# A two-layer trunk: token-major residual, nine seven-product units and a per-token shift in the first feed-forward block

## The chip, the core and the metric

One core of one Trainium2 chip runs the kernel. The metric is the device time of one execution in microseconds, as a median of several runs. Engines are named as in the profile: PE is TensorE, whose weight loads are shown as PEld; DVE is VectorE, ACT is ScalarE, POOL is GpSimd, SP is SyncE, which here issues DMAs. L164 means line 164 of the kernel.

## What is computed

A decoder trunk of two layers over one sequence of 256 tokens with 2048 features, in float32. Layer 0 mixes tokens by trailing means; layer 1 by attention in three dilated branches, with keys and values made of layer 0's output. Each layer ends in a gated feed-forward block (FFN) with a causal convolution of width 3 and 5504 hidden features, and each half ends in a layer norm over `ALPHA * h + f(h)`:

```
def conv_ffn(h, w_up, conv_w, conv_b, w_down):
    u = h @ w_up
    ...
    gate, val = jnp.split(c, 2, axis=-1)
    return (jax.nn.silu(gate) * val) @ w_down
...
        h = layer_norm(DEEPNORM_ALPHA * h + mix, ln1_g[i], ln1_b[i])
        ff = conv_ffn(h, ffn_w_up[i], ffn_conv_w[i], ffn_conv_b[i], ffn_w_down[i])
        h = layer_norm(DEEPNORM_ALPHA * h + ff, ln2_g[i], ln2_b[i])
```

The change touches `ff` of layer 0, the addition that follows, and the norm behind it.

## The kernel before, in words

**Units.** All weights pass through a list of units (`units`). A unit is a block of at most 512 x 512 weights with a function that issues its matmuls and one that runs behind them (`post`). `run_units` works through the list in order. Ahead of each unit, `ahead` issues the weight loads of up to five units to come on SP (L72) and splits those of up to three: ACT casts a block to fp32r (`wh`, L82), DVE takes the rest (`wl`, L83). Three raw buffers and four pairs of split ones bound this. A product of two float32 matrices is then three fp32r products: high by high, high by low, low by high. `later(n, f)` runs `f` behind the matmuls of the unit that comes n units later. So the order on every engine is the order in which the Python code issues instructions; each engine works strictly in its order, and a wait on one instruction holds back all behind it.

**Feature-major groups** (`group`, `mm_quad`, L149-186). Four row blocks of weights (three in the FFN's last down stage) add up into four PSUM banks, one for each 128 output features, with tokens along the free axis. In mode "ab" a matmul of 512 columns multiplies `wh` by the high and low part of the activations side by side, and one of 256 multiplies `wl` by the high part (L164, L165). Modes "a" and "x" take three matmuls of 256 or 258 columns (L167-169).

**Token-major groups** (`group_tm`, L188-268) hold 128 tokens in the partitions and 512 output features along the free axis: two PSUM banks, 24 matmuls of 512 columns for 512 rows of weights (L230-232).

**Seven block products.** In layer 1's FFN some units of the down projection use a scheme with seven products of half blocks in place of eight (`mk_seven`, L194-222; the table is `sevens`, L560). Such a unit takes two turns, "a" and "b", with 42 matmuls of 256 columns in all (L219-221). The weights' sums are made by DVE in `split_sums` (L90-108: two splits, L103, four sums, L105-108, and the split of the sums, L96); the activations' sums by `left_sums` (L619). Its results are put onto the residual by `early_post` (L724), in part by accumulating DMAs on POOL (L260).

**The FFN** (`ffn`, L556-697). It has eleven blocks q of 512 hidden features (the last has 384), each with a gate group and a value group of four row blocks. After blocks 2, 5, 7 and 10 comes a down stage over the blocks since the last one: three, three, two and three row blocks for each of the four groups c of 512 output features. The first two groups of a stage are interleaved (`turns`): a0 a1 b0 a2 b1 b2, then c0 c1 c2, d0 d1 d2. In layer 0 the down groups are feature-major: `resid_add` (L302) adds the PSUM banks to the residual H. In layer 1 the residual is moved to token-major layout at the FFN's start by `to_tokens` (L703: a DVE transpose of 32 x 32 blocks, L708, then sixteen DMAs on SP for the places of the blocks, L717), once for each c, and `tm_post` (L746) adds to it.

**The norm behind layer 0's FFN.** The last down stage runs `resid_last` (L315). For numerical safety a shift is taken off the residual ahead of the statistics: the mean over group 0's features, from a matmul with ones (`shift`, L364), which DVE subtracts from group 0, and which for the other groups enters their PSUM banks by one more matmul with `neg1` (L171). `stats` (L359) squares a group on ACT (L343) and folds it and its square over the free axis on DVE (L347, L349, L352). `xp` (L391) multiplies the not yet normalised residual by the norm's gain and splits it (L396, L397): it is what the first K group multiplies, one quarter for each of its four units, and the normalisation is applied behind that group (`norm_evac`, L443, L450, L452). `chain` (L402) sums the folds over partitions with two matmuls (L403, L404), makes the mean and the reciprocal deviation (L408-412), and then normalises the four quarters (L417, L418, L424) and splits them (L426, L274) into the operands XC, with which the query projection begins.

**Masks.** Three times, 30, 32 and 34 units behind the start of layer 0's FFN, `masks` (L1052) makes a 128 x 128 mask for the attention: an iota on POOL and ten DVE instructions (L1060-1067).

Of the kernel before, what the change touches and what calls it, by code (L numbers as in the profile page):

```python
# [32 lines left out]
def trunk(ctx: ExitStack, tc: tile.TileContext, x, pool_w_in, pool_w_grp, pool_scale, pool_w_out,  # L33
# [115 lines left out]
    def mm_quad(xq, ps, first, last, mode, mid, shifted):  # L149
        def go(h, l):  # L150
# [9 lines left out]
            for i, (k, m) in enumerate(order):  # L160
                c = slice(m * P, (m + 1) * P)
                st, sp = first and k == 0, last and k == nk - 1
                if mode == "ab":
                    PE.matmul(ps[m], h[:, k, c], q[:, k, :, :T], start=st, stop=False)  # L164
                    PE.matmul(ps[m][:, :T], l[:, k, c], q[:, k, 0, :T], start=False, stop=sp and not shifted)  # L165
                else:
                    PE.matmul(ps[m][:, :n], h[:, k, c], q[:, k, 0, :n], start=st, stop=False)  # L167
                    PE.matmul(ps[m][:, :n], h[:, k, c], q[:, k, 1, :n], start=False, stop=False)  # L168
                    PE.matmul(ps[m][:, :n], l[:, k, c], q[:, k, 0, :n], start=False, stop=sp and not shifted)  # L169
                if sp and shifted:  # L170
                    PE.matmul(ps[m][:, :T], neg1, ST["cs"], start=False, stop=True)  # L171
# [4 lines left out]
    def group(w, r0s, c0, ncol, xqs, post, mode="ab", mids=(), shifted=False):  # L176
        ps = []
        for j, (r0, nr) in enumerate(r0s):
            last = j == len(r0s) - 1
            units.append((w[r0:r0 + nr, c0:c0 + ncol],  # L180
                          mm_quad(xqs[j], ps, j == 0, last, mode, mids[j] if j < len(mids) else None, shifted),
                          (lambda: post(ps)) if last else None))
# [5 lines left out]
    def group_tm(w, r0s, c0, ncol, xqs, post, apart=False, seven=None, early=None):  # L188
# [5 lines left out]
        def mk_seven(kind):  # L194
            fin = len(r0s) == 2

            def go(h, l):
# [7 lines left out]
                def sm(i):  # L205
                    return lambda hl, kk: seven()[i][:, hl, kk, :]
# [82 lines left out]
    neg1 = const.tile([P, P], F32R, name="neg1")  # L289
# [12 lines left out]
    def resid_add(c, first):  # L302
        def post(ps):
            for m in range(4):
                y = H[c][:, m, :]
                if first:
                    V.scalar_tensor_tensor(y, y, ALPHA, ps[m][:, :T], op0=OP.mult, op1=OP.add)
                else:
                    V.tensor_tensor(y, y, ps[m][:, :T], OP.add)
            for m in range(4):  # L310
                y = H[c][:, m, :]
                V.tensor_tensor(y, y, ps[m][:, T:], OP.add)
        return post

    def resid_last(c, first, lay, which, after):  # L315
        def post(ps):
            for m in range(4):
                y = H[c][:, m, :]
                if first and c == 0:
# [7 lines left out]
            if c == 0:  # L327
                s = fold(H[0], None, "S0", F32R)
                later(1, lambda: shift(s, first, lay, which))
# [34 lines left out]
    def shift(s, first, lay, which):  # L364
        ps = bank("shift")
        PE.matmul(ps[:, :T], ones4, s, start=True, stop=True)
        cs = lnp.tile([P, T], F32R, name="cs", tag="cs")
        A.copy(cs, ps[:, :T])
        ST["cs"] = cs
        cb = cs.bitcast(F32).unsqueeze(1).to_broadcast([P, 4, T])  # L370
        ST["S"] = ST["Q"] = None

        def one():
            V.tensor_tensor(H[0], H[0], cb, OP.subtract)
            if first:
                pre(1)
            stats(0)

        def two():
            xp(0, lay, which)  # L380
            if first:
                pre(2)
                pre(3)
# [76 lines left out]
    def add_resid(w, rows, srcs, first):  # L460
        for c in range(4):
            group(w, rows, 512 * c, 512, srcs, resid_add(c, first))

    def add_last(w, rows, srcs, first, lay, which, after=None):
        for c in range(4):
            group(w, rows, 512 * c, 512, srcs, resid_last(c, first, lay, which, after),
                  mode="a" if c == 3 else "ab", shifted=c > 0 and not first)
# [66 lines left out]
    def add_grp(g):  # L534
# [12 lines left out]
             True, 0, 0)  # L547
# [8 lines left out]
    def ffn(lay):  # L556
# [3 lines left out]
        sevens = {0: (1, (0, 1, 2, 3)), 3: (4, (0, 1, 2, 3)), 6: (7, (2,)), 8: (9, (0, 2))} if lay == 1 else {}  # L560
# [58 lines left out]
        def left_sums(q, s):  # L619
            two = lnp.tile([P, 2, 2, 2, P], F32R, name="xs01", tag="sq")  # L620
            one = pools["ffn"].tile([P, 2, 2, P], F32R, name="xs2", tag="xs", bufs=1)
            if any(v[0] == q and len(v[1]) < 4 for v in sevens.values()):
                if "xs3" not in ST:
                    ST["xs3"] = hp.tile([P, 2, 2, 2, P], F32R, name="xs3", tag="h")
                own = ST["xs3"][:, 0]
            else:
                own = gq[q][:, 0:2, :, P:T].rearrange("p k h t -> p h k t")
# [479 lines left out]
```

## Time and profile before

| what | us |
|---|---|
| median of 3 runs | 2061.72 (2060.78 to 2063.05) |
| span of the profiled execution, first to last instruction | 2060.0 |
| PE busy | 2049.6 |
| DVE busy | 1505.6 |
| ACT busy | 1032.9 |
| POOL busy | 36.5 |

For the profiled execution the page gives the span alone. Matmuls overlap, and the ends of matmuls are modelled, so the time of a stage of PE's work is read from the start of its first matmul to the start of the first of the next stage. By this the first FFN's four down stages begin at 351.86, 554.18, 711.51 and 880.28 us of the span, and the K projection begins at 943.98. The second FFN's down stages begin at 1464.60, 1666.36, 1820.80 and 1988.38.

A row of the table of stretches has: the stretch, its length, PE's busy time in it with the number of matmuls that touch it, the granted clock, the share of the DMA engines' time and GB/s. A row of the timeline has: start, length, engine, line, operation, output and inputs, shapes, count. A row of waits has: who waited for whom, us in total, times, the longest.

### The profile page before, as it was taken

How to read it: one execution, taken by the hardware profiler on the slowest of the kernel's cores; microseconds unless marked ns; L12 is line 12 of the kernel's file. 1: busy time of each engine (PE TensorE's matmuls, PEld its weight loads, DVE VectorE, ACT ScalarE, POOL GpSimd, SP SyncE). 2: the span in 40 equal slices, each digit the busy share in tenths (PEclk: the TensorE clock that was granted, in tenths of full speed). 3: DMA queues.
4: the chain of work that ended last, by engine and by line, in shares of the span. 5: the costliest groups of instructions: out<-in, count | busy, mean ns of one | idle time of the engine just before them, and what ended most of it. 6: DMA issues, size and time to landing. Idle time of an engine off the chain costs nothing.

```text
span 2060.0 us, 29055 instructions
## 1 busy us (share of the span) xinstructions
PE 2049.6 (99%) x11942; PEld 1799.5 (87%) x11942; DVE 1505.6 (73%) x1925; ACT 1032.9 (50%) x1139; POOL 36.5 (2%) x67
## 2 busy tenths in 40 slices
PE   9999999999999999999999999999999999999998
PEld 8999988888888888889888888998888888888887
DVE  6768877756756766779755667788886787676688
ACT  6445665345534535547544344575445544544552
POOL 2000000000000000000000000000010001000000
PEclk9999999999999999999999999999999999999999
DMA  8655565655555555555566555556686558556554
GB/s 269 212 189 189 173 197 172 203 184 185 184 196 191 171 198 180 182 183 172 191 193 200 174 169 179 179 180 186 190 253 219 189 164 265 184 164 222 166 184 164
DMA packets 236997, 393.71 MB, mean 191 GB/s; under 512 B 44878, under 2 KB 56292, under 8 KB 236608
## 3 DMA queue, kind: packets, MB, share of 16 engines
q1 hardware_dynamic: 231328, 385.52, 57.4%
q0 software_dynamic: 5104, 5.69, 1.7%
q8 instruction: 93, 1.52, 0.3%
q10 hardware_dynamic: 432, 0.66, 0.1%
q14 instruction: 40, 0.33, 0.0%
HBM read 380.01 MB, written 2.10 MB: 185 GB/s over the span
## 4 chain that ended last, share of the span: by engine, by line
PE 91%; DVE 4%; DMA 2%; ACT 1%; issue 1%; SPq 0%; POOL 0%; DVEq 0%; ACTq 0%; POOLq 0%
PE acc L164 47%; PE acc L165 24%; PE t L231 3%; PE t L230 3%; PE t L232 3%; PE acc L168 3%; PE acc L169 3%; PE acc L167 3%; DVE wl L83 1%; DMA raw<-in_ffn_w_up_dram 1%; ACT wh L82 1%; DMA raw<-in_ffn_w_down_dram 1%; DMA ht<-u 0%; ACT wh L95 0%; DVE wl L96 0%
## 5 line engine op out<-in xcount | busy, mean ns | idle before, releaser
L164 PE MATMUL acc<-xc,wh 128*128 128x512 f32 x3264 | 1149.5, 396 | 0.0
L83 DVE TENSOR_TENSOR wl<-raw,wh 128x2048 fp32r<-128x2048 f32 (+2 forms) x365 | 795.5, 2184 | 405.2 <-ACT wh L82 395.5
L82 ACT CAST wh<-raw 128x2048 fp32r<-128x2048 f32 (+2 forms) x365 | 664.2, 1825 | 535.5 <-PE acc L164 346.7
L165 PE MATMUL acc<-xc,wl 128*128 128x256 f32 x3264 | 915.9, 281 | 0.0
L164 PEld LDWEIGHTS acc<-xc,wh 128*128 128x128 f32 x3264 | 615.7, 189 | 145.7 <-DVE o L959 0.6
L165 PEld LDWEIGHTS acc<-xc,wl 128*128 128x128 f32 x3264 | 615.5, 189 | 0.2
L164 PE MATMUL acc<-g,wh 128*128 128x512 f32 x644 | 226.8, 396 | 0.0
L165 PE MATMUL acc<-g,wl 128*128 128x256 f32 x644 | 180.6, 280 | 0.0
L164 PEld LDWEIGHTS acc<-g,wh 128*128 128x128 f32 x644 | 121.5, 189 | 28.4
L592 DVE SCALAR_TENSOR_TENSOR c<-u,cv,c 128x256 f32<-128x256 f32 x344 | 141.6, 478 | 0.5
L165 PEld LDWEIGHTS acc<-g,wl 128*128 128x128 f32 x644 | 121.7, 189 | 0.0
L579 ACT COPY ut<-acc 128x256 f32<-128x256 f32 x164 | 58.8, 371 | 95.7 <-PE acc L165 95.4
L231 PE MATMUL t<-wl,g 128*128 128x512 f32 (+1 forms) x267 | 102.8, 385 | 0.3 <-DVE wl L83 0.3
L230 PE MATMUL t<-wh,g 128*128 128x512 f32 (+1 forms) x267 | 103.0, 386 | 0.0
L232 PE MATMUL t<-wh,g 128*128 128x512 f32 (+1 forms) x267 | 102.6, 384 | 0.0
L588 ACT ACTIVATE c<-u,cv 128x256 f32<-128x256 f32 x172 | 89.6, 596 | 3.1 <-DVE u L580 3.1
L580 DVE TENSOR_TENSOR u<-acc,ut 128x256 f32<-128x256 f32 x164 | 60.9, 416 | 30.7 <-ACT ut L579 30.7
L164 PE MATMUL acc<-o,wh 128*128 128x512 f32 x192 | 67.9, 396 | 0.0
L164 PE MATMUL acc<-mixed,wh 128*128 128x512 f32 x192 | 67.5, 395 | 0.0
L278 ACT CAST g<-c 128x1024 fp32r<-128x1024 f32 (+1 forms) x22 | 22.6, 1029 | 84.4 <-DVE c L658 84.4
L231 PEld LDWEIGHTS t<-wl,g 128*128 128x128 f32 x267 | 50.2, 188 | 11.1 <-DVE wl L83 1.1
L232 PEld LDWEIGHTS t<-wh,g 128*128 128x128 f32 x267 | 50.1, 188 | 11.0
(265 smaller groups left out, 2358.7 us busy)
## 6 DMA issues: line engine op xcount, KB each, us to landing
raw<-in_ffn_w_up_dram SPq DMA_DIRECT2D x160, 1024.0 KB, 5.1
raw<-in_ffn_w_down_dram SPq DMA_DIRECT2D x80, 1024.0 KB, 5.1
raw<-in_pool_w_out_dram SPq DMA_DIRECT2D x16, 1024.0 KB, 5.0
raw<-in_shared_w_k_dram SPq DMA_DIRECT2D x16, 1024.0 KB, 5.1
raw<-in_attn_w_q_dram SPq DMA_DIRECT2D x16, 1024.0 KB, 5.2
raw<-in_shared_w_v_dram SPq DMA_DIRECT2D x16, 1024.0 KB, 5.8
raw<-in_attn_w_o_dram SPq DMA_DIRECT2D x16, 1024.0 KB, 5.0
raw<-in_pool_w_in_dram SPq DMA_DIRECT2D x12, 1024.0 KB, 5.7
```

The costliest lines, as they stand in the source:

```text
L82: A.copy(wh[i][:, s], r[:, s])
L83: V.tensor_tensor(wl[i][:, s], r[:, s], wh[i][:, s].bitcast(F32), OP.subtract)
L164: PE.matmul(ps[m], h[:, k, c], q[:, k, :, :T], start=st, stop=False)
L165: PE.matmul(ps[m][:, :T], l[:, k, c], q[:, k, 0, :T], start=False, stop=sp and not shifted)
L167: PE.matmul(ps[m][:, :n], h[:, k, c], q[:, k, 0, :n], start=st, stop=False)
L168: PE.matmul(ps[m][:, :n], h[:, k, c], q[:, k, 1, :n], start=False, stop=False)
L169: PE.matmul(ps[m][:, :n], l[:, k, c], q[:, k, 0, :n], start=False, stop=sp and not shifted)
L230: PE.matmul(to, xh, h[:, k, c], start=j == 0 and k == 0, stop=False)
L231: PE.matmul(to, xh, l[:, k, c], start=False, stop=False)
L232: PE.matmul(to, xl, h[:, k, c], start=False, stop=j == len(r0s) - 1 and k == nk - 1)
L588: A.activation(c[:, m, :], u[:, m, 2:], AF.Identity, scale=cv[:, 2, j:j + 1], bias=cv[:, 3, j:j + 1])
L592: V.scalar_tensor_tensor(c[:, m, :], u[:, m, i:i + T], cv[:, i, j:j + 1], c[:, m, :], op0=OP.mult, op1=OP.add)
```

## The change

Layer 0's FFN now does what layer 1's does, with a way back at its end:

- Its residual is moved to token-major layout at the FFN's start (`to_tokens` now also follows layer 0's first norm), and all its down groups are token-major.
- Nine of its down units take seven block products: all four groups in the first two stages, one in the third, none in the last.
- In the last stage `tm_post` takes the per-token mean of group 0 from an accumulating addition and subtracts it from each group. The shift matmuls, `neg1` and the arguments for them go.
- A group that is complete is moved back to feature-major layout by the new `to_features`: a DVE transpose, sixteen DMAs on SP one unit later, and `stats` one more unit later. For the last group `xp` and `chain` follow at once; `chain` has a PSUM bank of its own.
- The masks use buffers of the FFN's temporaries ("t1") and work in place; the fourth sums of the activations in units with fewer than four sevens use buffers of the norm's tags ("S" and "Q").

```diff
-    def resid_add(c, first):
...
-    def resid_last(c, first, lay, which, after):
+    def resid_last(c, lay, which, after):
...
-                n = 3 if c == 1 and not first else 1
-                later(n, lambda: stats(c))
-                later(n + 1, lambda: xp(c, lay, which))
+                later(1, lambda: stats(c))
+                later(2, lambda: xp(c, lay, which))
...
-                if sp and shifted:
-                    PE.matmul(ps[m][:, :T], neg1, ST["cs"], start=False, stop=True)
...
-    def add_last(w, rows, srcs, first, lay, which, after=None):
+    def add_last(w, rows, srcs, lay, which):
         for c in range(4):
-            group(w, rows, 512 * c, 512, srcs, resid_last(c, first, lay, which, after),
-                  mode="a" if c == 3 else "ab", shifted=c > 0 and not first)
+            group(w, rows, 512 * c, 512, srcs, resid_last(c, lay, which, lambda q: to_tokens(q)),
+                  mode="a" if c == 3 else "ab")
...
-        sevens = {0: (1, (0, 1, 2, 3)), 3: (4, (0, 1, 2, 3)), 6: (7, (2,)), 8: (9, (0, 2))} if lay == 1 else {}
+        sevens = {0: (1, (0, 1, 2, 3)), 3: (4, (0, 1, 2, 3)), 6: (7, (2,)), 8: (9, (0, 2))}
+        if lay == 0:
+            del sevens[8]
...
-            if lay == 1:
...
-            elif last:
-                add_last(w_dn, rows, srcs, False, 0, 1)
-            else:
-                add_resid(w_dn, rows, srcs, qs[0] == 0)
+            sq, cs7 = sevens.get(qs[0], (None, ()))
+            for c in range(4):
+                group_tm(w_dn, rows, 512 * c, 512, srcs, tm_post(lay, c, qs[0] == 0, last),
+                         apart=lay == 1 and last and c == 3, seven=(lambda: xs[sq]) if c in cs7 else None,
+                         early=early_post(c, not last))
...
+    def to_features(c):
+        hb = hp.tile([P, 4, T], F32, name="hb", tag="h")
+        hf = hb.rearrange("p m t -> p (m t)")
+        V.transpose(hf.rearrange("p (m t c) -> p t m c", m=4, t=2), HT[c].rearrange("p t (m c) -> p t m c", m=4))
+
+        def move():
+            H[c] = hp.tile([P, 4, T], F32, name="h", tag="h")
+            to = H[c].rearrange("p m t -> p (m t)").rearrange("p (k a j) -> p a k j", k=8, a=4)
+            fr = hf.rearrange("p (k b j) -> p b k j", k=8, b=4)
+            for a in range(4):
+                for b in range(4):
+                    nc.sync.dma_start(to[32 * b:32 * b + 32, a], fr[32 * a:32 * a + 32, b])
+
+        def use():
+            if c == 0:
+                ST["S"] = ST["Q"] = None
+            stats(c)
+            if c == 3:
+                xp(3, 0, 1)
+                chain(bank("st"), 0, 1, None)
+            else:
+                later(1, lambda: xp(c, 0, 1))
+
+        later(1, move)
+        later(2, use)
...
-    def tm_post(c, first, last):
+    def tm_post(lay, c, first, last):
...
+            if lay == 0 and last:
+                if c == 0 and t == 0:
+                    ST["m0"] = lnp.tile([P, 2], F32, name="m0", tag="m0")
+                m0 = ST["m0"][:, t:t + 1]
+                if c == 0:
+                    V.scalar_tensor_tensor(y, ps, 1.0, y, op0=OP.mult, op1=OP.add, accum_out=m0)
+                    V.tensor_scalar(m0, m0, 1.0 / 512, None, op0=OP.mult)
+                    V.tensor_scalar(y, y, m0, None, op0=OP.subtract)
+                else:
+                    V.scalar_tensor_tensor(y, ps, m0, y, op0=OP.subtract, op1=OP.add)
+                if t == 1:
+                    to_features(c)
+                return
...
         def masks(i):
-            dist = fp.tile([P, P], F32, name="dist", tag="dist", bufs=1)
+            two = fp.tile([P, 2, P], F32, name="dist", tag="t1", bufs=4)
+            dist, fm = two[:, 0], two[:, 1]
...
-            idist = fp.tile([P, P], I32, name="idist", tag="idist", bufs=1)
-            im = fp.tile([P, P], I32, name="im", tag="im", bufs=1)
-            fm = fp.tile([P, P], F32, name="fm", tag="fm", bufs=1)
+            itwo = fp.tile([P, 2, P], I32, name="idist", tag="t1", bufs=4)
+            idist, im = itwo[:, 0], itwo[:, 1]
```

More of the change, by code (lines that the diff above doesn't have):

```diff
@@ L147, in trunk, with mm_quad @@
     XW = T + 2
-    def mm_quad(xq, ps, first, last, mode, mid, shifted):
+    def mm_quad(xq, ps, first, last, mode, mid):
         def go(h, l):
@@ L380, in two @@
             xp(0, lay, which)
[L381 to L383 removed]
+            pre(2)
+            pre(3)
         def pre(q):
@@ L965, in trunk @@
         group_tm(shared_w_v, rows4, 512 * hq, 512, xsrcs, v_post(hq))
-    add_last(attn_w_o[0], rows4, [lambda j=j: oq[j] for j in range(4)], True, 1, 0, after=to_tokens)
+    add_last(attn_w_o[0], rows4, [lambda j=j: oq[j] for j in range(4)], 1, 0)
     marks.append(len(units))
```

63 lines of the change are left out of this document (18 added, 45 removed).

## The prediction

> **What bounds the kernel now.** I read the page's busy shares, then its chain of waits, then a table of stretches, one for each stage that the change touches.
>
> ```profile
> span 2060.0 us, 29055 instructions
> PE 2049.6 (99%) x11942; PEld 1799.5 (87%) x11942; DVE 1505.6 (73%) x1925; ACT 1032.9 (50%) x1139; POOL 36.5 (2%) x67
> ...
> PE 91%; DVE 4%; DMA 2%; ACT 1%; issue 1%; SPq 0%; POOL 0%; DVEq 0%; ACTq 0%; POOLq 0%
> ```
>
> TensorE (PE) is busy in 2049.6 of 2060.0 us and holds 91% of the chain that ended last. So a change gains what it takes out of PE's stream, and loses what PE newly waits for. Only one execution's span is shown; the median of the runs, 2061.72, lies 1.7 above it. I add changes to the span and give the result 1.7 higher.
>
> The stretches below are cut at the first matmul that reads "g" (a down stage begins) and the first that reads something else. The upper four are the first FFN's down stages, which I call D1 to D4; then come D1 to D3 of the second FFN, which is token-major already and has seven-product units; the last is two token-major units of the V projection.
>
> ```profile
> core 0: us, PE busy (x), PEclk, DMA share, GB/s
> ...
> 351.86:419.24 67.38, 67.38 (x386) 1.00 0.57 188
> 554.18:621.56 67.38, 67.38 (x386) 1.00 0.56 187
> 711.51:756.54 45.03, 45.03 (x258) 1.00 0.56 187
> 880.28:943.98 63.70, 63.70 (x412) 1.00 0.52 174
> ...
> 1464.60:1531.52 66.92, 65.41 (x362) 1.00 0.69 213
> 1666.36:1730.90 64.54, 64.54 (x362) 1.00 0.70 217
> 1820.80:1864.74 43.94, 43.94 (x212) 1.00 0.61 191
> 990.75:1001.93 11.18, 11.18 (x50) 1.00 0.60 200
> ```
>
> A plain token-major unit (512 weight rows) takes 11.18 / 2 = 5.59 us. D2 with four seven-product units takes 64.54 where D2 without takes 67.38.
>
> **The change part by part.** *Seven-product units, D2 and D3.* The second FFN shows the same stages as the first will have: D2 gains 67.38 - 64.54 = 2.84, D3 (one such unit) 45.03 - 43.94 = 1.09.
>
> *D4* gets no seven products. Its four groups become token-major units of 512, 512 and 384 rows: 5.59 + 5.59 + 4.19 (three quarters) = 15.37, four times 61.5 against 63.70, which held twelve small shift matmuls. Gain 2.2.
>
> *D1* is not its twin's equal, because the attention masks stay where they are. In the second FFN's D1, PE is idle for 1.5 of 66.92 us, and weight loads wait for VectorE (DVE):
>
> ```profile
> PEld t L220 <- DVE wl L96: 1.6, 2, 1.2
> PEld t L231 <- DVE wl L83: 1.1, 2, 0.6
> ```
>
> The waits sum to 2.7 us: DVE delivers just in time there, since a seven-product unit costs it more splits and sums. In the first FFN's D1 the three mask blocks stand in the same places of DVE's order. One block runs from its first to its last row, 384.20 to 386.59:
>
> ```profile
> 384.20 0.22 DVE L1060 CAST idist<-dist 128x128 int32<-128x128 f32 x1
> ...
> 386.36 0.23 DVE L1067 TENSOR_SCALAR negm<-cnt 128x128 f32<-128x128 f32 x1
> ```
>
> That is 2.4 us, 7.2 for three. Today the stage has no seven-product units and DVE hides them; without that cover they cost 0 to 7.2. In the changed order one stands behind the first group's sums, and two more before the last seven-product unit. PE's waits are few and short there, so DVE catches up between them and absorbs a part; I take 4.5, nearer to 7.2 because DVE had no lead where PE did wait. D1 then takes 66.92 + 4.5 = 71.4, a loss of 4.0 (bounds: a gain of 0.5, a loss of 6.7).
>
> The four moves to token-major layout at the FFN's start (64 DMAs, SP) are those that stand before the second FFN's D1, so the 66.92 contains their harm.
>
> *The way back, D4 to the K projection.* This decides. Each column group of D4 now ends in: two additions, a DVE transpose, sixteen DMAs on SP, and statistics (squares, folds) that read what the DMAs wrote. No row of before has this way back; its mirror image, to_tokens of the second layer, has sixteen DMAs of equal size each:
>
> ```profile
> 1394.48 10.40 SPq L717 DMA_DIRECT2D ht<-hb  x16
> ...
> 1410.87 13.34 SPq L717 DMA_DIRECT2D ht<-hb  x16
> ...
> 1426.94 16.08 SPq L717 DMA_DIRECT2D ht<-hb  x16
> ...
> 1445.98 14.19 SPq L717 DMA_DIRECT2D ht<-hb  x16
> ```
>
> ```profile
> DMA to landing us min/median/max: 1.9/2.0/10.4
> ```
>
> SP issues sixteen in 10.4 to 16.1 us, and the last lands 2.0 after its issue. The longer ones followed loads issued just before them, for whose queue they waited. In the changed order the loads ahead of each move are mostly landed, so I take the shortest: 10.4 + 2.0 = 12.4 for a move (upper end 18.1).
>
> Could four such moves lie beside PE's work? The order of DVE's instructions in the changed program says no: the statistics of group c stand ahead of the additions of group c+1, and DVE works strictly in its order. So each transpose waits until the move before it has landed. The other instructions of the loop have these rows:
>
> ```profile
> L708 DVE STREAM_TRANSPOSE hb<-h x4: 1236/1242/1246, 1393.2 to 1444.7; 128x1024 f32<-128x1024 f32 x4
> ```
>
> ```profile
> L752 DVE SCALAR_TENSOR_TENSOR ht<-ht,t x8: 680/680/681, 1492.1 to 1538.3; 128x512 f32<-128x512 f32 x8
> ```
>
> ```profile
> L83 DVE TENSOR_TENSOR wl<-raw,wh 128x2048 fp32r<-128x2048 f32 x325 | 743.4, 2290 | 385.7 <-ACT wh L82 383.7
> ...
> L83 DVE TENSOR_TENSOR wl<-raw,wh 128x1536 fp32r<-128x1536 f32 x24 | 42.1, 1754 | 19.5 <-ACT wh L82 11.8 <-PE acc L165 7.7
> ...
> L397 DVE SCALAR_TENSOR_TENSOR xp<-h,vec,xp 128x256 fp32r<-128x256 f32 x48 | 20.0, 479 | 0.0
> ...
> L343 ACT ACTIVATE sq<-h 128x512 f32<-128x512 f32 x24 | 14.5, 628 | 29.1 <-DVE h L322 12.4 <-DVE h L374 10.0 <-DVE h L324 6.7
> ...
> L347 DVE TENSOR_TENSOR fold<-h 128x512 f32<-128x512 f32 x15 | 10.3, 689 | 0.2
> ```
>
> ```profile
> L349 DVE TENSOR_TENSOR S<-fold x15: 424/425/427, 155.9 to 1329.7; 128x256 f32<-128x256 f32 x12, 128x256 fp32r<-128x256 f32 x3
> ```
>
> ```profile
> L352 DVE TENSOR_TENSOR S<-S x9: 424/426/428, 180.8 to 1330.1; 128x256 f32<-128x256 f32 x9
> ```
>
> Let zero be the end of D4's fourth unit, which completes group 0 (the first two groups are interleaved). DVE's additions for one group are two of 0.68, and the transpose is 1.24. Group 0 also subtracts its mean; I take that at the addition's 0.68 and 0.1 for scaling the mean, so 2.7 to the first transpose's end. Move 0 lands at 15.1. Two squares (2 x 0.63), the fold of the squares (0.69 + 0.42), group 1's additions (1.36) and transpose (1.24): 5.0, to 20.1. Move 1 lands at 32.5. Folds with running sums (2 x 1.54 = 3.1), the split of a 384-row unit (1.75), four products for the K input (4 x 0.48 = 1.9), additions and transpose (2.6): 9.35, to 41.9. Move 2 lands at 54.3. Folds 3.1, a full split 2.29, products 1.9, additions and transpose 2.6: 9.9, to 64.2. Move 3 lands at 76.6, its folds end at 79.7. Then the two matmuls can run that sum the statistics over partitions; in PE's order they stand between the second and the third K unit.
>
> What PE has to do meanwhile: units of 5.59 and 4.19, groups 2 and 3 at 15.37 each, and two K units. These are known from:
>
> ```profile
> 943.98:949.73 5.75, 5.75 (x50) 1.00 0.87 318
> 950.41:967.92 17.51, 17.51 (x146) 1.00 0.38 122
> ```
>
> The second of these stretches holds three K units (5.84 each), the first one of 5.75, so two cost 11.5. PE's work is 52.0 us, and it waits 79.7 - 52.0 = 27.7 us in all: a few at the last D4 unit and the first K unit, whose splits stand behind moves 1 and 2 on DVE, the rest ahead of the statistics matmuls. SP's weight loads queue behind the moves too, but each is due later than the DVE instruction that it feeds is free.
>
> *Behind the statistics.* The query projection needs the normalised stream. Today three K units (17.51) lie between the statistics matmuls and it; after the change two (11.5). The path in between, today:
>
> ```profile
> 954.70 1.75 DVE L411 RECIPROCAL rm<-rm 128x256 f32<-128x256 f32 x1 [0.58 <-ACT rm L410]
> ...
> 966.55 1.22 DVE L274 TENSOR_TENSOR xc<-h,xc 128x1024 fp32r<-128x1024 f32 x1
> ...
> 984.27 0.75 DVE L450 TENSOR_TENSOR qt<-acc,rm 128x256 f32<-128x256 f32 x2
> 984.94 0.87 DVE L452 SCALAR_TENSOR_TENSOR qt<-rm,wgb,qt 128x256 f32<-128x256 f32 x2
> ```
>
> ```profile
> 951.28 1.28 ACT L410 ACT_TABLE_LOAD   x1
> ...
> 954.15 0.51 ACT L410 ACTIVATE rm<-rm,epst 128x256 f32<-128x256 f32 x1 [1.58 <-DVE rm L409]
> ```
>
> From 950.41 to the end of the first low part at 967.77 it takes 17.4 us, and hides within 17.51. In the changed order no weight split stands ahead of the variance, so the reciprocal can start 2.4 behind the matmuls instead of 4.3 (a square no longer than the 0.63 above, the table load, the root of 0.51): the path is 15.5, and PE waits 15.5 - 11.5 = 4.0 (from 2 to 6). The K group's normalisation, four pairs of instructions of 0.75 + 0.87 by two, 3.2 in all, now stands ahead of the last low part: 2.0 more (0 to 3.2). Together 6.0.
>
> *The clock.* Ten equal warm matmuls at the kernel's start took 2.50 us, four of the same from 4.46 on only 0.62:
>
> ```profile
> 1.06 2.50 PE L992 MATMUL warm<-one 128*128 128x128 f32 x10 [1.06 <-DVE one L988]
> ...
> 4.46 0.62 PE L1003 MATMUL warm<-one 128*128 128x128 f32 x4
> ```
>
> So for 3.4 us after idling, TensorE runs at about half pace and loses 1.7 us of work. The page grants full clock everywhere else, as PE never idles long. The Trainium skill, "TensorE: Matmul & The Clock Gate" (Part 1 on idle windows), says that an idle stretch of about 3.4 us puts the clock back to half until it has been busy as long. The start agrees; no row here has a long idle stretch mid-kernel. By that rule the third K unit would start cold. In my sum this costs nothing more, because the 1.7 lies in the 4.0 for which the query projection waits anyway; without that wait it would be 1.7.
>
> *At nothing:* the removed neg1 set-up, buffers under other tags, and the statistics' own bank (PE and DVE order show them outside any wait). If a buffer were not free in time, it would show as a DVE wait of a unit's length.
>
> **The sum:** -2.84 - 1.09 - 2.2 + 4.0 + 27.7 + 6.0 = +31.6; 2060.0 + 31.6 = 2091.6 of span, 2093 as a run.
>
> **Rivals.** (1) *The moves are hidden after all, and it gets faster.* PE's 52.0 us cover the loop if the four moves together take no more than 52.0 - 30.1 (all DVE terms) = 21.9, thus 5.5 each. Then the gains remain, with D1 as in its twin: -2.84 - 1.09 - 2.2 - 0.5 = -6.6, a run of 2055. Against it: no move was shorter than 10.4 in issue alone. For it: only that four moves were seen. 4%, and 2% for landing within 4.1 us of today between the two.
> (2) *The moves are as slow as the later three of the twin* (mean 14.5 of issue): 4 x 4.1 = 16.6 more, 2109. For it: loads do stand on SP directly ahead of the moves. 24%.
> (3) *The edges are mild:* masks absorbed by DVE's idle time and the query projection hardly late: 31.6 - 4.5 - 5 = 22, a run of 2083. For it: the twin's D1, where DVE is late for moments only. 20%.
> The forecast (2086 to 2100) has 50%.
>
> **How the numbers follow.** 2093 is the forecast's time. The range 2078 to 2110 takes in rivals 2 and 3 and leaves out the hidden moves and the far end of slow ones. About 0.2%, 4.1 us, is what a measurement of this kernel can tell from no change: faster 4%, same 2%, slower 94%.
>
> **What would show it.** D2 of the first FFN at 64.5 and D3 at 43.9; D4 with no shift matmul. DVE idle four times for 10 us or so between D4's middle and the second K unit, each ended by a DMA that writes h. PE idle for over 15 us ahead of the statistics matmuls. DVE, not PE, ending waits in D1. It would be wrong if the sixteen DMAs take 5 us, or if the trace shows the transposes running without waiting for the move before them.

## The result and the profile after

| | before | changed |
|---|---|---|
| median of 5 runs each, us | 2063.04 (2060.78 to 2064.28) | 2093.37 (2092.59 to 2096.05) |
| ratio | | 1.0156, 95% interval [1.0143, 1.0168] |
| span of the profiled execution, us | 2060.0 | 2090.9 |

The change costs 30 us; the forecast was 2093. Lines of the changed kernel's page, as those quoted of before:

```profile
PE 2048.7 (98%) x11703; PEld 1788.7 (86%) x11703; DVE 1551.1 (74%) x1957; ACT 1052.0 (50%) x1176; POOL 59.7 (3%) x94
...
PE   9999999999999999995899999999999999999998
...
PEclk9999999999999999997999999999999999999999
...
PE 68%; DVE 7%; DMA 2%; SPq 2%; ACT 2%; issue 1%; DVEq 0%; POOL 0%; ACTq 0%; POOLq 0%
```

TensorE (PE) has almost the same work (2048.7 against 2049.6 us), and the span is 30.9 longer: what was added is waiting. It lies in two of the 40 slices (the "5" and the "8" behind it), that is from 940 to 1045 us, and the granted clock dips there. The chain of waits now runs through SyncE's queue (SPq), which had 0% before.

The same stretches as in the prediction, cut in the same way (columns: length, PE busy with its instructions, granted clock, DMA share, GB/s):

```profile
core 0: us, PE busy (x), PEclk, DMA share, GB/s
351.86:422.08 70.22, 65.71 (x363) 1.00 0.66 196
557.02:621.34 64.32, 64.32 (x363) 1.00 0.66 201
711.29:755.38 44.09, 44.09 (x213) 1.00 0.61 193
879.09:942.30 63.21, 61.53 (x266) 1.00 0.59 170
942.30:978.00 35.70, 13.46 (x97) 0.73 0.52 134
978.00:980.18 2.18, 1.88 (x4) 0.50 1.05 407
980.18:996.24 16.06, 12.94 (x98) 0.93 0.36 119
996.24:1023.96 27.72, 24.41 (x129) 0.94 0.54 177
1497.80:1563.01 65.21, 65.03 (x363) 1.00 0.69 211
```

In order: D1 to D4 of the first FFN; the first two K units with the wait behind them; the statistics matmuls; the third and fourth K unit with a wait behind them; the first query group; D1 of the second FFN. The fifth row is the loss: 35.70 us of which PE works 13.46.

Who waits for whom from 880 to 1024 us (engine and line, what released it; sum, times, longest):

```profile
DVE fold L330 <- DMA h<-hb: 29.1, 4, 8.1
...
PE st L383 <- DVE S L335: 20.4, 1, 20.4
...
PE acc L164 <- DVE xc L272: 6.4, 2, 3.3
...
PE acc L169 <- DVE wl L83: 1.9, 1, 1.9
```

Four times VectorE (DVE, its folds) stands still for the DMA that turns a group back, and PE then stands 20.4 us ahead of the statistics. The last of the four moves, from SP's timeline, and the link between the third move and the last, from DVE's:

```profile
964.36 10.40 SPq L705 DMA_DIRECT2D h<-hb  x16
```

```profile
954.81 0.69 DVE L330 TENSOR_TENSOR fold<-h 128x512 f32<-128x512 f32 x1 [8.09 <-DMA h<-hb]
...
963.08 1.25 DVE L697 STREAM_TRANSPOSE hb<-ht 128x1024 f32<-128x1024 f32 x1
```

Sixteen DMAs take 10.4 us to issue, and in DVE's order each transpose stands behind the folds that wait for the move before.

### The profile page after: what moved, and what is told of

It is laid out like the page before. It is cut to its first block, busy times and chain, and to the rows that moved or that the text cites. A ratio compares the mean times of both kernels' runs of the same rounds, so it can differ in the third digit from the quotient of the medians.

```text
span 2090.9 us, 28892 instructions
## 1 busy us (share of the span) xinstructions
PE 2048.7 (98%) x11703; PEld 1788.7 (86%) x11703; DVE 1551.1 (74%) x1957; ACT 1052.0 (50%) x1176; POOL 59.7 (3%) x94
## 4 chain that ended last, share of the span: by engine, by line
PE 68%; DVE 7%; DMA 2%; SPq 2%; ACT 2%; issue 1%; DVEq 0%; POOL 0%; ACTq 0%; POOLq 0%
PE acc L164 31%; PE acc L165 16%; PE t L229 5%; PE t L230 5%; PE t L228 5%; SPq L705 2%; DVE wl L83 2%; DMA raw<-in_ffn_w_down_dram 1%; ACT wh L82 1%; PE acc L168 1%; PE acc L169 1%; PE acc L167 1%; ACT wh L95 1%; DVE wl L103 1%; PE s L219 0%
## 5 line engine op out<-in xcount | busy, mean ns | idle before, releaser
L164 PE MATMUL acc<-xc,wh 128*128 128x512 f32 x3264 | 1150.8, 396 | 6.4 <-DVE xc L272 6.4
L83 DVE TENSOR_TENSOR wl<-raw,wh 128x2048 fp32r<-128x2048 f32 (+2 forms) x356 | 774.1, 2181 | 349.7 <-ACT wh L82 341.1
L82 ACT CAST wh<-raw 128x2048 fp32r<-128x2048 f32 (+2 forms) x356 | 647.0, 1822 | 445.9 <-PE acc L164 203.4
L164 PEld LDWEIGHTS acc<-xc,wh 128*128 128x128 f32 x3264 | 616.5, 189 | 152.7 <-issue 3.6
L229 PE MATMUL t<-wl,g 128*128 128x512 f32 (+1 forms) x539 | 210.3, 390 | 4.5 <-DVE wl L83 4.5
L228 PE MATMUL t<-wh,g 128*128 128x512 f32 (+1 forms) x539 | 210.4, 390 | 0.0
L230 PE MATMUL t<-wh,g 128*128 128x512 f32 (+1 forms) x539 | 209.8, 389 | 0.0
L229 PEld LDWEIGHTS t<-wl,g 128*128 128x128 f32 x539 | 101.4, 188 | 27.4 <-DVE wl L83 5.9
L230 PEld LDWEIGHTS t<-wh,g 128*128 128x128 f32 x539 | 101.2, 188 | 23.1
L228 PEld LDWEIGHTS t<-wh,g 128*128 128x128 f32 x539 | 101.2, 188 | 22.1
L95 ACT CAST wh<-raw 128x2048 fp32r<-128x2048 f32 x20 | 38.2, 1910 | 85.2 <-DVE raw L108 72.5
L164 PE MATMUL acc<-o,wh 128*128 128x512 f32 x192 | 67.9, 397 | 0.0
L164 PE MATMUL acc<-mixed,wh 128*128 128x512 f32 x192 | 67.5, 395 | 0.0
L258 POOL DMA_DIRECT2D ht<-w x18 | 15.3, 849 | 1809.6 <-DVE ht L763 1155.4
L96 DVE TENSOR_TENSOR wl<-raw,wh 128x2048 fp32r<-128x2048 f32 x20 | 45.8, 2292 | 18.0 <-ACT wh L95 18.0
```

Source lines behind the costliest of these rows:

```text
L82: A.copy(wh[i][:, s], r[:, s])
L83: V.tensor_tensor(wl[i][:, s], r[:, s], wh[i][:, s].bitcast(F32), OP.subtract)
L95: A.copy(h, r)
L228: PE.matmul(to, xh, h[:, k, c], start=j == 0 and k == 0, stop=False)
L229: PE.matmul(to, xh, l[:, k, c], start=False, stop=False)
L230: PE.matmul(to, xl, h[:, k, c], start=False, stop=j == len(r0s) - 1 and k == nk - 1)
```

## The experiments

Unless said otherwise a kernel is the changed one with the edit shown. The kernel before ran beside each batch; ratios are to it.

| kernel | median us | ratio [95%] | span us |
|---|---|---|---|
| changed | 2093.37 | 1.0156 [1.0143, 1.0168] | 2090.9 |
| e1_order | 2089.93 | 1.0133 [1.0118, 1.0148] | 2086.3 |
| e2_masks | 2091.53 | 1.0141 [1.0126, 1.0156] | 2087.6 |
| e3_pe | 2074.30 | 1.0058 [1.0043, 1.0073] | 2072.6 |
| e4_queues | 2085.18 | 1.0116 [1.0099, 1.0132] | 2082.0 |
| e5_warm | 2105.23 | 1.0211 [1.0197, 1.0225] | 2106.1 |
| e6_pe_masks | 2070.73 | 1.0037 [1.0025, 1.0050] | 2069.0 |
| e7_x_q | 2057.59 | 0.9978 [0.9969, 0.9987] | 2054.5 |
| e8_late | 2058.64 | 0.9983 [0.9974, 0.9992] | 2056.9 |
| e9_warm_less | 2097.55 | 1.0169 [1.0154, 1.0184] | 2092.9 |
| e10_x_q | 2086.07 | 1.0118 [1.0101, 1.0135] | 2082.5 |
| e11_no_seven | 2093.49 | 1.0152 [1.0137, 1.0167] | 2094.2 |
| e12_parts | 2062.21 | 0.9998 [0.9989, 1.0007] | 2060.3 |

The theory: four moves, chained by DVE's order, make PE wait; behind the statistics the path to the normalised parts has lost a K unit of cover; D1 pays for the masks. The rivals: SP's queue holds up the weights; the clock, half after idling, is a cost of its own; the sevens themselves are what D1 pays for.

### What chains the moves: e1_order, e4_queues, e3_pe

*e1_order* issues the statistics later, behind the next groups' additions and transposes:

```diff
-        later(2, use)
+        later((3, 4, 4, 2)[c], use)
```

> The statistics of groups 0, 1 and 2 are issued one or two units later, so that on DVE the next group's additions and transpose stand ahead of them; the four moves keep their sixteen DMAs on SP. Theory (a chain of four moves held together by DVE's order): the moves start at PE's pace, the last one lands about 55.5 us behind the end of group 0, its folds end at 58.6 against 52.0 us of PE's work, so PE waits about 7 us ahead of the statistics matmuls instead of 22, and the time falls by 20 us to about 2072. Rival (the moves hold up the weight loads on SP): PE then waits for splits, and the time stays above 2082. Rival (each move is itself what PE waits for, wherever it stands): no change, 2093.

Measured 2089.93: a miss by some 18 us. The order of DVE was one link of several: PE's wait ahead of the statistics fell from 20.4 to 15.8 us. Its waits, and the last two moves on SP's timeline:

```profile
ACT wh L82 <- DMA raw<-in_shared_w_k_dram: 19.0, 2, 9.9
...
PE st L383 <- DVE S L335: 15.8, 1, 15.8
...
DVE hb L697 <- DMA h<-hb: 6.7, 2, 5.7
```

```profile
932.53 15.59 SPq L705 DMA_DIRECT2D h<-hb  x16
...
951.47 14.05 SPq L705 DMA_DIRECT2D h<-hb  x16
```

Now the transpose itself waits for an earlier move (DVE hb, 6.7 us: its target is a buffer of the tag "h", of which one comes free only when a move has landed), and the moves fill SP's queue so closely that two loads of K weights, issued behind a move, come late (19.0 us of the casts' time). SP holding up the weights, which the prediction had set aside for its own order of DVE, is a real rival as soon as the moves are denser.

*e4_queues* shares each move between two issuers:

```diff
-                    nc.sync.dma_start(to[32 * b:32 * b + 32, a], fr[32 * a:32 * a + 32, b])
+                    (nc.sync, nc.scalar)[b % 2].dma_start(to[32 * b:32 * b + 32, a], fr[32 * a:32 * a + 32, b])
```

> The sixteen DMAs of a move are issued by turns from SP and ACT, eight each; nothing else changes. Theory (a move's 10.4 us are the issue time of one sequencer): a move takes 5.2 + 2.0 = 7.2 us, the loop 30.1 + 4 x 7.2 = 58.9 against 52.0, PE waits 7 us in all instead of 27, the time falls by 20 to about 2073. Rival (the DMA engines' own time sets the move): a move stays at 10 us or more and the time at 2090 or above. ACT loses 5 us a move for issuing, which could delay its casts by some us: up to 2078 by the first theory.

Measured 2085.18, a miss by 12. The third move on SP's timeline, then on the scalar engine's, then on DVE's:

```profile
937.85 5.18 SPq L705 DMA_DIRECT2D h<-hb  x8
```

```profile
937.86 5.51 ACTq L705 DMA_DIRECT2D h<-hb  x8
943.46 1.92 ACT L82 CAST wh<-raw 128x2048 fp32r<-128x2048 f32 x1 [10.92 <-DMA h<-hb]
```

```profile
945.41 2.29 DVE L83 TENSOR_TENSOR wl<-raw,wh 128x2048 fp32r<-128x2048 f32 x1 [5.41 <-ACT wh L82]
```

The issue time did halve, so it is the issuer's, not the 16 DMA engines'. But the issue stands in the scalar engine's order ahead of a weight cast. That engine is done at 932.5, waits till 937.8 for DVE's transpose, issues for 5.5, and only then casts: 10.9 us without work (the profile names a DMA there, but issuing is not counted as busy). DVE, which splits that block next, waits 5.41 for the cast. A new chain, from DVE over the scalar engine and back, has taken the place of the old one. The Trainium skill, "DMA: Bandwidth & Descriptors" (Issuing engines are not separate DMA queues), says that issuing from several engines saves only the time to initiate the DMAs, usually small relative to the DMA. The first half agrees. The second does not hold for these: issuing one takes 0.61 us and sixteen in a row 10.39, against 2.0 us from the issue of one to its landing (medians of the changed kernel).

*e3_pe* turns the groups back on PE, as eight 128x128 transposes and two copies by the scalar engine; no DVE transpose, no DMA:

```diff
-        V.transpose(hf.rearrange(...), HT[c].rearrange(...))
...
-            for a in range(4):
-                for b in range(4):
-                    nc.sync.dma_start(...)
+            for half in range(2):
+                ps = bank("hT")
+                for kk in range(2):
+                    m = 2 * half + kk
+                    for t in range(2):
+                        PE.transpose(ps[:, kk * T + t * P:kk * T + t * P + P], HT[c][:, t, m * P:m * P + P], ident)
+                A.copy(H[c][:, 2 * half:2 * half + 2, :], ps.rearrange("p (k t) -> p k t", k=2))
```

> The way back to feature-major layout is made by PE: eight 128x128 transposes per group behind the next unit's matmuls, and two copies by ACT, instead of the DVE transpose and sixteen DMAs. Theory (the moves' round trips): the 27 us of waiting go, four times 0.8 us of transposes come, and 0 to 4 us remain ahead of the statistics matmuls; what follows them stays (9 us). Time about 2069, from 2066 to 2073. Rival (waits for splits or for DVE itself cause the loss): over 2080.

Measured 2074.30, just above the expected band. K0 and K1 with one set of transposes between them, the statistics, K2 and K3 with the wait behind them, the query group:

```profile
943.98:957.18 13.20, 12.59 (x105) 1.00 0.52 163
957.18:959.05 1.87, 1.05 (x4) 1.00 0.86 319
959.05:974.91 15.86, 11.89 (x99) 1.00 0.31 94
974.91:1003.94 29.03, 25.69 (x129) 0.88 0.54 180
```

35.70 us (K0 and K1 with the wait) have become 13.20. So the round trip by DVE and DMA is the wait ahead of the statistics: shown. What stands behind the statistics has not shrunk (3.97 us idle at the end of the third row, 29.03 in the query group against 27.72), which is the second cost, and a separate one.

### Behind the statistics, the path or the clock: e5_warm, e9_warm_less, e10_x_q

The granted clock in the changed kernel, cut finely around the two short waits (the statistics behind the long one have 0.50 in the table of stretches):

```profile
944.30:947.80 3.50, 3.23 (x16) 0.59 0.37 53
...
995.00:999.00 4.00, 2.76 (x9) 0.64 0.68 225
```

Three times PE runs at about half clock: behind a wait of 1.9 us (inside the first K unit), behind the long one, and behind one of 3.1 us ahead of the query group. *e5_warm* fills the long wait and the one ahead of the query group with matmuls of a constant that nothing reads:

```diff
+    def keep(n):
+        w = bank("warm")
+        for i in range(n):
+            PE.matmul(w[:, :P], one1, one1, start=True, stop=True)
...
+                keep(150)
                 chain(bank("st"), 0, 1, None)
+                later(2, lambda: keep(22))
```

> As the changed kernel (2093.4 us), with TensorE given idle work in two places: 150 matmuls 128x128 of a constant ahead of the statistics, which start when the last K unit before them is done and so run through the wait for the last move and the folds, and 22 more ahead of the first query unit. They compute nothing that is used. In the changed kernel the records show half-clock stretches at 961.0-981.5 (0.53, 0.50) and 995.0-999.0 (0.64), behind idle times of 20.4 and 3.1 us. Theory 'the clock costs': the statistics go back from 2.18 us to about 0.7 and the two K units behind them keep full pace, the query stage loses its slow first 3.4 us: span down by 2 to 4 us, time about 2090. Rival 'the clock costs nothing, since the vector engine ends last there': the statistics get quicker by 1.5 us, but the query stage waits that much longer for its XC parts: span the same within 1 us, time about 2093. If the warm matmuls themselves run longer than the wait, the time goes up.

```profile
991.19:991.87 0.68, 0.68 (x6) 1.00 0.00 0
991.87:1003.60 11.73, 11.73 (x98) 1.00 0.08 16
1003.60:1008.43 4.83, 4.83 (x46) 1.00 0.65 201
1008.43:1036.17 27.74, 24.42 (x132) 0.94 0.57 187
```

My 150 matmuls were too many (33.5 us instead of the 20.4 of the wait), so the time went up to 2105 and says nothing. The stretch says a little. With PE warm the statistics take 0.68 instead of 2.18 us and the K units 11.73 instead of 12.94 of work, 2.7 less together. Yet from the start of the statistics to the end of the query group it is 44.98 us (4.83 of it idle work) against 45.96 in the changed kernel. The rest was lost in two ways. The 22 matmuls ahead of the query group ended at 1008.43, 0.9 behind the end of the first low part (1007.57 in this trace). And PE's wait within the query group, 3.3 us as before, now left the clock low behind it, so that the group's work is as long as before (24.42 against 24.41). So the slow clock costs about 1 us there at least; how much more, this run does not show.

*e9_warm_less*: `keep(85)`, and none ahead of the query group.

> As e5_warm with 85 idle matmuls instead of 150 ahead of the statistics and none ahead of the query stage: in e5_warm one of them took 0.223 us, so that 150 ran 33.5 us, past the end of the wait; 85 take 19.0 us, just under the 20.4 us of the wait. Theory 'the slow clock costs': statistics 0.7 us instead of 2.2, the two K units behind them 11.7 instead of 16.1, all of it kept: about -5, 2088. Rival 'behind the statistics the normalised parts end last': the K units are quicker but the query stage waits longer for its first parts; only the statistics' 1.5 us stay, about 2092. In e5_warm the stretch from the statistics to the end of the query stage was only 1 us shorter than in the changed kernel, for which the rival is the likelier.

```profile
975.95:977.97 2.02, 0.04 (x2) 1.00 0.79 202
977.97:980.15 2.18, 1.36 (x5) 0.66 1.05 409
```

It did not test what it should: 2.0 us idle ahead of the statistics were enough to bring the clock down, and they took 2.18 us again. So neither theory was tested. The time, 2097.55, lies above both expectations and 4 us above the changed kernel's; of the 2.0 that its span grew, 1.45 lie in the query group (29.17 us):

```profile
1000.00:1004.00 4.00, 4.00 (x23) 1.00 0.50 151
1004.00:1025.37 21.37, 18.00 (x87) 0.84 0.50 169
```

Here the clock was full at first and fell behind its second wait instead (0.84 in the last row). Each wait of 2 to 3 us may bring such a stretch, and which one does differs from kernel to kernel.

*e10_x_q* takes away the path's due time instead. The first query group is multiplied from the residual before normalisation, as the first K group is, and normalised in its eviction; the normalised parts are first needed by the V units:

```diff
-        group(attn_w_q[0], rows4, 512 * hq, 512, xsrcs, qk_post("q", hq))
+        group(attn_w_q[0], rows4, 512 * hq, 512, psrcs if x0 else xsrcs, qk_post("q", hq), mode="x" if x0 else "ab")
...
-            if hq == 0 and nm == "k":
+            if hq == 0:
                 norm_evac(ps, 4, tmp, lambda m: o[:, m, :])
```

> The changed kernel with only the first query block taken from the residual that is not yet normalised, as in e7_x_q; moves by DMA and masks as in the changed kernel. Theory: what was charged behind the statistics goes, and the wait ahead of them stays: query stage 23.2 instead of 27.7 us, K units behind the statistics 11.7 to 16.1 (their part is the clock's after the long wait, and XP's): -5 to -9, 2084 to 2088. Rival, the wait is only put off to the value block: within 2 us of the changed kernel, 2091 to 2093.

Measured 2086.07, in the band. The statistics, then K2, K3 and the whole query group in one row:

```profile
977.45:979.63 2.18, 1.88 (x5) 0.50 1.05 404
979.63:1015.72 36.09, 36.09 (x290) 0.96 0.41 139
```

From the statistics to the end of the query group: 38.27 us instead of 45.96. PE never idles in the last row, and the slow clock in it and in the statistics, which is still there, costs about 1.3 and 1.5. The V units behind it do not wait either, so nothing was only put off. The path to the normalised parts, with the slow stretch that its own wait brings, is shown to be the cost there (7.7 us); the slow clock behind the long wait is the smaller part.

### D1, masks or sevens: e2_masks, e11_no_seven

*e2_masks* moves the mask building away from D1:

```diff
-            later(30 + 2 * i, lambda i=i: masks(i))
+            later(50 + 2 * i, lambda i=i: masks(i))
```

> The three mask blocks are issued 50, 52 and 54 units behind the start of the first FFN instead of 30, 32 and 34, so behind its first down stage. Theory (the masks, without cover, cost that stage PE time): its length falls from 70.2 us to what the second FFN's twin has, 65.2 to 66.9, and the time to 2088.5 to 2090. Rival (the stage is late because of the moves to token-major layout before it): it stays at 70 and the time at 2093.

*e11_no_seven* leaves the masks and takes the nine sevens out (`sevens = {}` for the first FFN).

> The changed kernel without seven products in the first FFN (its nine units take eight block products again), all else as changed. If their gain is what the trace shows in the second and third down block (3.06 + 0.94 us) and the first block's surplus is the masks' alone, the second and third give back 4.0 and the first another 0 to 3: 2097 to 2100. Rival: the first block's surplus is due to the vector work that the sevens add beside the masks; then its stretch falls from 70.2 to about 67 and the time is 2094 to 2095.

Measured 2091.53 and 2093.49. The first is 1.5 above the band that was expected, and its runs (2089.38 to 2093.05) overlap those of the changed kernel (2092.59 to 2096.05), so the reading rests on the stretches and waits, not on the time. PE's waits in D1 of the changed kernel:

```profile
PE t L229 <- DVE wl L83: 2.7, 2, 2.5
PE t L218 <- DVE wl L96: 1.8, 2, 1.2
```

That is 4.5 us for DVE's weight splits; it is 1.3 in e2_masks, and nothing in e11_no_seven and in the kernel before. D1 of e2_masks, then D1 to D3 of e11_no_seven:

```profile
352.10:418.60 66.50, 65.23 (x362) 1.00 0.71 215
```

```profile
352.26:419.18 66.92, 66.92 (x290) 1.00 0.65 221
554.20:621.10 66.90, 66.90 (x290) 1.00 0.57 188
711.10:755.80 44.70, 44.70 (x195) 1.00 0.56 188
```

D1 takes 70.22 with both, 66.50 without the masks, 66.92 without the sevens: neither is dear alone, and together they are more than DVE can hide. The rival of e11_no_seven holds: its time equals that of the changed kernel, since the sevens gain 66.90 - 64.32 = 2.58 in D2 and 0.61 in D3 and lose 3.30 in D1. As the change places them, nine sevens bring nothing.

### Putting it together: e6_pe_masks, e7_x_q, e8_late, e12_parts

*e6_pe_masks* is e3_pe with the masks of e2_masks.

> The two earlier edits together: transposes on TensorE in place of vector transpose and 64 DMAs (alone 2074.3 us, -19.1), and the mask building moved from unit 30 to unit 50 of the stage (alone -1.8 in the time, -3.3 in the span). If the two causes are separate, about 2071 (2069 to 2073); if the masks land on the chain behind the statistics, no gain, 2074.

Measured 2070.73: the two causes are separate. *e7_x_q* adds the edit of e10_x_q.

> As e6_pe_masks, and the first query block too is taken from the scaled, not yet normalised residual (three products of 258 columns, normalised behind the matmuls as the first key block is), so that the normalised parts are not needed before the value block, some 23 us later. In e3_pe the records behind the statistics show TensorE idle 3.9 us ahead of the query stage, 1.4 and 1.9 us inside it, and a clock of 0.62 to 0.81 behind each. Theory 'what is left is the chain from the statistics to the normalised parts': those go, the query stage costs about 23.2 us instead of 29.0 and the K units 11.6 instead of 15.9: about 9 us less than e6_pe_masks, some 2062 (2060 to 2064), level with the kernel before (2062.5). Rival 'vector and scalar engines are full there, so that the wait is only put off to the value block': 2066 to 2071.

```profile
952.17:954.04 1.87, 1.05 (x4) 1.00 0.91 310
954.04:965.60 11.56, 11.56 (x97) 1.00 0.15 45
965.60:988.82 23.22, 23.22 (x195) 1.00 0.53 178
```

Measured 2057.59, ratio 0.9978 [0.9969, 0.9987]: faster than the kernel before, by 4 us, and 2.4 below the band that was expected. From the statistics (first row) to the end of the query group (last) it is 36.65 us, at full clock, with no wait but 0.8 us between the matmuls of the statistics; the same stretch took 46.76 us in e3_pe.

*e8_late* puts the statistics behind the third K unit: `later(1, lambda: chain(bank("st"), 0, 1, None))`.

> As e7_x_q, with the statistics' matmuls behind the third K unit instead of the second, so that TensorE does not wait for the last folds (0.6 and 0.8 us in e3_pe, 1.87 us for the statistics instead of 0.7). Expected 1 to 1.5 us below e7_x_q if the value block still has its parts in time, about 2061, which would be just under the kernel before; if the parts are then late, up to 3 us above e7_x_q.

Measured 2058.64: not the gain that was expected; its runs (2057.06 to 2060.66) overlap those of e7_x_q (2056.29 to 2059.39). In the profiled execution the statistics take 0.68 us instead of 1.87, but its span is 2.4 longer: PE waits 1.3 us for DVE in the attention's outputs (L164 behind L968), 0.6 for a DMA there and 1.0 at a down stage, all of which e7_x_q does not. That the shift causes these was not tested.

*e12_parts* is e7_x_q with `sevens = {}` for the first FFN.

> As e7_x_q without seven products in the first FFN: what is left is the token-major residual and the per-token shift, with transposes on TensorE and the query block ahead of its normalisation. Theory: with the masks out of the first block, the sevens bring what the second and third block show (2.6 and 0.6 us between the changed kernel and e11_no_seven) and up to 1 us in the first, and the residual's layout brings nothing: 3 to 4 us above e7_x_q, about 2061, level with the kernel before. Rival: the layout by itself brings the gain and the sevens nothing, as in e11_no_seven: 2058, as e7_x_q.

Measured 2062.21, ratio 0.9998 [0.9989, 1.0007]. The token-major residual with the per-token shift, once its way back is cheap, neither gains nor loses; the nine sevens are worth the 4 us, if D1 does not have to carry the masks too.

## Why the prediction was right

The time (2093.37 against 2093.0) and the span's growth (30.9 against 31.6) agree. The largest term was right; that the total agrees to 1 us is luck, because errors of 1 to 3.5 us in the others cancelled. Term by term, in us:

| term | predicted | measured |
|---|---|---|
| D1 | +4.0 | 70.22 - 67.38 = +2.8 |
| D2, D3 | -2.84, -1.09 | -3.06, -0.94 |
| D4's own work | -2.2 | 61.53 of work against 63.70: -2.2 |
| wait up to the statistics | +27.7 | 1.7 in D4, 35.70 - 11.5 = 24.2, and 1.5 in the statistics: +27.4 |
| behind the statistics | +6.0 | 16.06 - 11.5 = 4.6 and 27.72 - 22.8 = 4.9: +9.5 |
| second FFN's D1 | 0 | 65.21 - 66.92 = -1.7 |

The measured terms add up to 31.9, 1.0 more than the span grew; 0.6 of that lies behind the second FFN's D1 (527.9 us to the end against 528.5 before), the rest is rounding.

- **The way back.** Right in mechanism and size. Zero of the sum (the end of group 0's last unit) is at 900.1; the last folds were to end 79.7 behind it and ended at 979.5, 79.4 behind. Choosing the shortest issue time (10.4) was right for this order: SP held few loads ahead of the moves (10.39, 10.39, 11.10, 10.40). It holds for this order only: in e1_order, with the moves closer together, the last two took 15.59 and 14.05, as in the rival of slow moves.
- **D1.** The mechanism, masks beside sevens on DVE, is shown by two experiments from both sides and by PE's waits there. The size, 4.5 for the masks, was too high: e2_masks gives 70.22 - 66.50 = 3.7.
- **Behind the statistics.** The waits agree in sum (3.1 ahead of the query group and 3.3 within it, against 6.0), but not in their parts. Ahead of the query group it is 4.6 against 4.0: the first low part is done 15.9 us behind the statistics (980.18 to 996.10) against 15.5, and the third K unit's cold start lies inside that wait, so the step "in my sum this costs nothing more" held there. Within the query group it is 4.9 against 2.0. The term that was mis-sized is the K group's normalisation ahead of the last low part. DVE's third low part and its last (the low halves of the normalised quarters, xc), changed and then before:

```profile
1007.67 1.22 DVE L272 TENSOR_TENSOR xc<-h,xc 128x1024 fp32r<-128x1024 f32 x1
...
1014.64 2.29 DVE L83 TENSOR_TENSOR wl<-raw,wh 128x2048 fp32r<-128x2048 f32 x1 [2.44 <-ACT wh L82]
1016.85 1.22 DVE L272 TENSOR_TENSOR xc<-h,xc 128x1024 fp32r<-128x1024 f32 x1
```

```profile
978.01 1.22 DVE L274 TENSOR_TENSOR xc<-h,xc 128x1024 fp32r<-128x1024 f32 x1
...
983.14 1.22 DVE L274 TENSOR_TENSOR xc<-h,xc 128x1024 fp32r<-128x1024 f32 x1
```

From one to the other it is 9.2 us where it was 5.1, so 4.1 more: DVE's 3.4 us of the normalisation come in full, and the wait for a weight cast, which on the scalar engine stands behind that engine's own share of the normalisation, is 2.4 where it was 1.7. The forecast had not seen two effects of the clock. The statistics matmuls, which head the path, were cold too (2.18 for 0.68). And the wait of 3.1 us made the query group's start cold: the cast that needs the buffer of its first unit came later, and DVE waited 1.2 for it ahead of the third low part. In e9_warm_less, where the query group starts at full clock, DVE does not wait there. In all, half clock makes 4.5 us of slow work (1.5 in the statistics, 1.4 in the K units, 1.6 in the query group), part of it inside waits; what it costs by itself stays open between that and the 1 us of e5_warm.
- **The second FFN's D1**, which the change does not touch, was not in the sum. It took 65.21 here and 66.92 before; in e3_pe, e5_warm and e7_x_q, with the same code there, it took 67.2, 68.1 and 64.7. It moves by a few us with what precedes it; I have no cause for it.
- **The rivals.** Hidden moves: excluded by the 29.1 us for which DVE waited for them. Slow moves: excluded here, real in e1_order. Mild edges: excluded, since behind the statistics it was worse than forecast.

The Trainium skill, "TensorE: Matmul & The Clock Gate" (Why this matters for your kernels), holds that there should be no idle gap of more than about 3 us between bursts. The traces here are stricter: half clock came behind 3.1 us, and behind 2.0 (e9_warm_less) and 1.9 us too; yet in e5_warm the same 1.9 us in the first K unit were followed by full clock. Part 1 of that page says that the window in which activity is judged runs freely, so the moment of a wait could matter; no run here varied the moment of one wait by itself.

## What to carry to other kernels

A change of layout pays where its way back is cheap: price the round trip (here 10.4 us of issue and 2.0 of landing per group by DVE and DMA, 0.8 us per group on PE and 1.1 of copies on the scalar engine in e3_pe) against the work that must cover it, and look in the order of each engine for what chains one trip to the next, since taking out one link (e1_order) or halving one (e4_queues) left the others standing. An edit that costs nothing where an engine has room costs in full where another edit has just used that room up: masks and sevens were free alone and took 3.3 to 3.7 us together. When a path behind a reduction becomes too long for its cover, moving its due time (a consumer that can take the value before normalisation) took the cost away: 7.7 us here, in e10_x_q. Whether the path itself could be made faster was not tried.

## What the runs showed that I had not expected

- Idle times of 1.9 to 3.1 us were followed by about 3.5 us at half clock (0.59, 0.66, 0.64 in the rows above), though not always.
- Eight transposes 128x128 of 4-byte values on PE, amid matmuls, take 0.79 us, less than two of the sixteen DMAs need to be issued (0.61 each).
- The DMAs' issue is the issuer's own time: 16 on one took 10.39 us, 8 on each of two 5.19 and 5.53.
